# Values of a head pair in one chain of half-width products, latent sample scores in another

## The chip, the cores and the metric

The kernel runs on one core of a Trainium2 chip. The metric is the device time of one launch in microseconds; smaller is better. TensorE (PE) multiplies, PEld is its weight load, VectorE (DVE), ScalarE (ACT) and GpSimd (POOL) do the elementwise work, and SyncE (SP) issues the transfers. Each engine takes its instructions in a fixed order, and waits for semaphores where an operand comes from another engine.

## The reference

One inference step of a two-layer encoder in fp32, for 256 frames of a new stream ("prompt") and 64 frames of a running stream ("sample"), 320 columns together. Each layer is a SwiGLU block, a mixer stage and a second SwiGLU block, each followed by a layer norm. The mixer stage has two kinds of attention with eight heads of 64 values each, latent (A) and banded (B):

```python
# A, sample: 512 cached latent rows and the 64 new ones are keys and values
keys_c = jnp.concatenate([cache_ckv, ckv], axis=1)
s = (einsum('bqhc,bkc->bhqk', q_abs, keys_c) + einsum('bqhr,bkr->bhqk', q_rope, keys_r)) * MLA_SCALE
p = jax.nn.softmax(s, axis=-1)
o = einsum('bhqk,bkc->bqhc', p, keys_c)            # prompt: same, with a chunk mask
# B: own chunk of 64 and the 8 before it, with a learned relative bias
s = einsum('bqhd,bkhd->bhqk', q, k) * BAND_SCALE + bias
o = einsum('bhqk,bkhd->bqhd', softmax(s), v)
mix = (sigmoid(g_a) * (o_a @ w_pa) + sigmoid(g_b) * (o_b @ w_pb)) @ w_out
```

So per pair of heads there are scores, a softmax and values, for the sample (576 keys) and for the prompt (256 keys), in both A and B.

## The kernel before, in words

Activations lie with features on the 128 partitions and the 320 frames along the free dimension, as blocks of 128 features. Weights stream through SP's queue into staging tiles `wst`, and each is split into a high part `whi` (ACT, line 81) and a low part `wlo` (DVE, every sixth on POOL, line 83). A projection multiplies each 128 x 128 weight block three times (`mm3`: high by high, high by low, low by high), each a 128 x 320 product of type fp32r. They are by far the most instructions on TensorE, and are called weight products below.

Scores, transposes of probabilities and values are fp32 products. Heads come in pairs: head j of a pair owns partitions j*64 to j*64+63 of the results. Full-width products give 128 partitions at once (`sp`, the prompt scores, and `ss` in attention B, with zeros in Q to keep the heads apart). Half-width ones give 64 partitions, one head: the sample values (tile `so`, 64 columns), the prompt values (`po`, 256 and 128 columns) and, in attention A alone, the sample scores (`ss`, 288 columns, two halves b of two heads j each).

For each pair, `values_sample` transposes the sample's probabilities into PSUM tiles `st0`, `st1`, copies them to `pts` (ACT, line 586) and `ptn` (DVE, line 587) and multiplies: five products for each head, heads alternating. `hi` and `lo` (lines 123 and 130) then split the 64 columns into `oh` (ACT) and `ol` (DVE), the operands of the output projection. `values_prompt` does the same with `pt0`, `pt1`, `pt` (ACT line 566, DVE line 567) and four products, into 256 columns of the same `oh` and `ol`. That is six PSUM tiles of the tag "at" for a pair.

The program is written as a sequence of such steps, with projections between them. A list scheduler then sets each engine's order: it takes what it reckons to be ready, in order of priority, so products from different steps are mixed. What it sets is fixed before the run; on the chip each engine keeps to it and waits where its reckoning was wrong. Layer 0's mixer stage lies at about 265 to 505 us of the trace, layer 1's at 1030 to 1280. In each, B's four pairs come first (`values(0)` to `values(3)`), then A's four (`mla_pair`, `mla_scores`, `mvalues`). `mla_pair(i)` forms a pair's Q (a memset on POOL, DMAs of the rotary part, products on DVE) and K (copies on ACT and DVE); `mla_scores` multiplies them.

Of the kernel before, what the change touches and what calls it, by code (L numbers as in the profile page):

```python
# [23 lines left out]
PAST = 512  # L24
# [24 lines left out]
class WeightStream:  # L49


    def __init__(self, nc, dram, stage_pool, split_pool, ahead_dma, ahead_split):
        self.nc, self.dram = nc, dram
        self.sp, self.pp = stage_pool, split_pool
        self.ad, self.asp = ahead_dma, ahead_split
        self.order = []
        self.loaded = {}
        self.split = {}
        self.nl = self.ns = self.nlo = 0
# [42 lines left out]
class Model:  # L102
    def __init__(self, tc, a):
        self.tc, self.nc, self.a = tc, tc.nc, a


    def mm(self, out, lhsT, rhs, start, stop):
        self.nc.tensor.matmul(out, lhsT, rhs, start=start, stop=stop)  # L108

    def mm3(self, out, w, x, start, stop):  # L110
        self.mm(out, w[0], x[0], start, False)
# [341 lines left out]
class Mixer:  # L453
# [100 lines left out]
                nc.vector.tensor_scalar(pr[j][:, c0:c1], pr[j][:, c0:c1], st[:, 12 + i:13 + i], None, ALU.mult)  # L554
        return pr

    def values_prompt(self, pr, vp, i, o):
        nc, M = self.nc, self.M
        p0 = M.psum("at", "pt0")
        p1 = M.psum("at", "pt1")  # L560
        for j in range(2):
            nc.tensor.transpose(p0[:, j * 256:j * 256 + 128], pr[j][:, 256:384], M.ident)
            nc.tensor.transpose(p0[:, j * 256 + 128:j * 256 + 256], pr[j][:, 0:128], M.ident)
            nc.tensor.transpose(p1[:, j * 128:j * 128 + 128], pr[j][:, 128:256], M.ident)
        pt = self.tile([P, 768], F32, "pt", 2)
        nc.scalar.copy(pt[:, 0:512], p0)
        nc.vector.tensor_copy(pt[:, 512:768], p1[:, 0:256])
        ps = M.psum("at", "po")
        c = [slice(i * 128 + j * 64, i * 128 + j * 64 + 64) for j in range(2)]
        for j in range(2):  # L570
            M.mm(ps[j * 64:j * 64 + 64, 0:256], vp[0][:, c[j]], pt[:, j * 256:j * 256 + 256], True, False)
        for j in range(2):
            M.mm(ps[j * 64:j * 64 + 64, 128:256], vp[1][:, c[j]], pt[:, 512 + j * 128:640 + j * 128], False, True)
        M.hi(o[0][:, TS:T], ps[:, 0:256])
        M.lo(o[1][:, TS:T], ps[:, 0:256], o[0][:, TS:T])

    def values_sample(self, pr, vc, vs, i, o):

        nc, M = self.nc, self.M
        p0 = M.psum("at", "st0")  # L580
        p1 = M.psum("at", "st1")
        for t in range(4):
            nc.tensor.transpose(p0[:, t * 128:t * 128 + 128], pr[:, t * 128:t * 128 + 128], M.ident)
        nc.tensor.transpose(p1[0:64, 0:128], pr[:, 512:576], M.ident)
        pt = self.tile([P, 512], F32, "pts", 1)
        nc.scalar.copy(pt, p0)
        nc.vector.tensor_copy(M.ptn[0:64, :], p1[0:64, 0:128])
        ps = M.psum("at", "so")
        pairs = [(vc[t], pt[:, t * 128:t * 128 + 128]) for t in range(4)] + [(vs, M.ptn)]
        for t, (v, x) in enumerate(pairs):  # L590
            for j in range(2):
                r = slice(j * 64, j * 64 + 64)
                M.mm(ps[r, 0:64], v[:, r], x[:, r], t == 0, t == 4)
        M.hi(o[0][:, 0:TS], ps[:, 0:64])
        M.lo(o[1][:, 0:TS], ps[:, 0:64], o[0][:, 0:TS])

    def normalise_sample(self, pr, st, n):
        nc = self.nc
# [123 lines left out]
    def mla_pair(self, i):  # L722

        nc, M, l = self.nc, self.M, self.l
        pq = self.uq(i)
        Q = self.tile([P, 640], F32, "Q", 4)
        nc.gpsimd.memset(Q[96:128, 0:T], 0.0)
        nc.gpsimd.memset(Q[0:32, T:], 0.0)
        for j, (r, n) in enumerate(((64, 0), (32, 64))):
            t, g = divmod(2 * i + j, 4)  # L730
            c = slice(j * T, j * T + T)
            nc.sync.dma_start(out=Q[r:r + 32, c], in_=self.qr[t][g * 32:g * 32 + 32, :])
            nc.vector.tensor_tensor(Q[n:n + 64, c], pq[n:n + 64, :T], self.rq[n:n + 64, :], ALU.mult)
        w = [self.ws.next(("uk", l, i, k)) for k in range(2)]
        p0, p1 = M.psum("mm"), M.psum("mm")
        for k in range(2):
            M.mm3(p0, w[k], self.cc[k], k == 0, k == 1)
        for k in range(2):
            M.mm3(p1[:, :T], w[k], self.ckv[k], k == 0, k == 1)
        K = self.keys[i % 2]  # L740
        for k, r in zip(K, (slice(0, 64), slice(64, 128))):
            nc.scalar.copy(k[r, 0:PAST], p0[r, :])
            nc.vector.tensor_copy(k[r, PAST:], p1[r, 0:T])
        return Q, K

    def mla_scores(self, i, Q, K):
        nc, M = self.nc, self.M
        s = [M.psum("at", "ss") for _ in range(2)]
        for b in range(2):
            c = slice(b * 288, b * 288 + 288)  # L750
            for j in range(2):
                M.mm(s[b][j * 64:j * 64 + 64, 0:288], Q[:, j * T:j * T + TS], K[j][:, c], True, True)
        st = self.tile([P, 16], F32, "st", 8)
        pr = self.tile([P, 576], F32, "ps", 2)
        for b in range(2):
            nc.vector.tensor_reduce(st[:, b:b + 1], s[b][:, 0:288], AX.X, ALU.max)
        nc.vector.tensor_scalar(st[:, 2:3], st[:, 0:1], st[:, 1:2], -MLA_SCALE, ALU.max, ALU.mult)
        for b in range(2):
            nc.scalar.activation(pr[:, b * 288:b * 288 + 288], s[b][:, 0:288], AF.Exp, bias=st[:, 2:3], scale=MLA_SCALE,
                                 accum_out=st[:, 4 + b:5 + b])  # L760
        self.normalise_sample(pr, st, 2)
        sp = self.scores_prompt([Q[:, j * T + TS:j * T + T] for j in range(2)], K)
        for p in sp:
# [29 lines left out]
    def attention(self, pre):  # L793
        nc, M, l, a, ws = self.nc, self.M, self.l, self.a, self.ws
# [13 lines left out]
        Q = {}  # L808
        for i in range(2):
            Q[i] = self.band_q(*pre[2 * i])  # L810
            t, b = pre[2 * i + 1]
            self.band_k(i, t, ld[i][0], b)
        pv = [M.psum("at") for _ in rows]
        for i in range(NPAIR):
            ps = self.w_in("bv", i, "mm")
# [5 lines left out]
        vs = M.vsn  # L821
        nc.scalar.copy(vs[0:TS, :], pv[0][:TS, :])
        vp = [self.new_values(pv[t]) for t in (1, 2)]
# [6 lines left out]
        ob = [[self.tile([P, TR], F32R, f"o{n}{i}", 1) for n in "hl"] for i in range(NPAIR)]  # L830
# [5 lines left out]
        def values(i):  # L836
            prs, prp = S.pop(i)
            vc = ld[i][1]
            self.values_sample(prs, [vc[:, t * 128:t * 128 + 128] for t in range(4)], vs[:, i * 128:i * 128 + 128], i, ob[i])
            self.values_prompt(prp, vp, i, ob[i])  # L840

        def prep(i):
            ld[i] = self.band_load(i)
# [6 lines left out]
        scores(1)  # L850
        self.latent_kv()
        values(0)
        prep(3)
        scores(2)
        for j in range(3):
            self.latent_q(j)
        values(1)
        scores(3)
        for j in range(3, 6):
            self.latent_q(j)  # L860
        gb[0] = self.gate(1, 0)
        values(2)
        for m in range(1, 4):
            gb[m] = self.gate(1, m)
# [28 lines left out]
        vsm = M.vsn  # L893
        nc.scalar.copy(vsm[0:TS, :], pn[0][:TS, :])
        vpm = [self.new_values(pn[t]) for t in (1, 2)]
        H[1] = self.mla_pair(1)
        oa = [[self.tile([P, TR], F32R, f"o{n}{i}", 1) for n in "hl"] for i in range(NPAIR)]

        def mvalues(i):
            prs, prp = S.pop(i)  # L900
            c = slice(i * 128, i * 128 + 128)
            self.values_sample(prs, [v[:, c] for v in vcm], vsm[:, c], i, oa[i])
            self.values_prompt(prp, vpm, i, oa[i])

        mscores(1)
        ga[0] = self.gate(0, 0)
        mvalues(0)
        H[2] = self.mla_pair(2)
        mscores(2)
        ga[1] = self.gate(0, 1)  # L910
        mvalues(1)
        H[3] = self.mla_pair(3)
        mscores(3)
        ga[2] = self.gate(0, 2)
        mvalues(2)
        for m in range(3, 8):
            ga[m] = self.gate(0, m)
# [137 lines left out]
```

## Time and profile before

| | |
|---|---|
| median of 3 runs | 1546.58 us (1546.03 to 1548.86) |
| profiled execution | 1545.9 us, span 1544.1 us, granted clock 0.991 |
| busy, share of the span | PE 97%, PEld 94%, DVE 59%, ACT 48%, POOL 36% |
| PE idle, layer 0's mixer stage (265 to 505) | 7.0 of 240 us |
| PE idle, layer 1's mixer stage (1030 to 1280) | 5.2 of 250 us |

The span is what the trace covers; the rest of an execution's time lies around it. A row of the timeline has start, length (to the modelled end of the last of them), engine, line, operation, tile written <- tiles read, shape and the number of records merged into the row. Weight products overlap, so the time one takes is read from the start of the next, not from its length. Line 108 is the helper that issues all products, so they are told apart by their tiles. A product in fp32 has two records. Shapes with 128*64 are half width.

### The profile page before, as it was taken

To read this page: it belongs to the slowest core of one execution; us is meant where nothing else is said; L and a number is where in the kernel's file an instruction comes from. 1 tells how busy PE (TensorE), PEld (TensorE's weight loads), DVE (VectorE), ACT (ScalarE), POOL (GpSimd) and SP (SyncE) were. 2 spreads that over 40 slices of the span, in tenths; PEclk is the share of its full clock that TensorE was granted. 3 is DMA by queue.
4 is the path that set the end of the run, shared out by engine and by line. 5 is a ranking of instruction groups with operands and counts; after the bars stand their busy time and mean duration, and the time that the engine had idled before them with its cause. 6 is when DMAs were issued, how large, how long until landed. Compare 5 with 4: busy or idle time off the path is not lost. (4 is left out here: it accounts for less than half of the span.)

```text
span 1544.1 us, 26702 instructions
## 1 busy us (share of the span) xinstructions
PE 1499.4 (97%) x10207; PEld 1454.2 (94%) x10207; DVE 904.7 (59%) x1603; ACT 747.0 (48%) x1579; POOL 562.0 (36%) x602
## 2 busy tenths in 40 slices
PE   9999999999999899999999999999999999999996
PEld 9999999899898899999999999998998998899996
DVE  6333368775466994333784333786745579933345
ACT  5444345765453554443554443466634545544332
POOL 7222235232004683222483222452220146722234
PEclk9999999999999999999999999999999999999998
DMA  7554445844323435444435444457343334454441
GB/s 227 160 152 150 148 126 170 248 135 132 96 83 96 149 99 177 150 150 151 144 117 164 143 157 149 139 171 233 112 131 96 97 109 124 139 162 151 150 137 62
DMA packets 69920, 219.46 MB, mean 142 GB/s; under 512 B 8416, under 2 KB 17568, under 8 KB 69792
## 3 DMA queue, kind: packets, MB, share of 16 engines
q1 hardware_dynamic: 69792, 217.75, 45.5%
q8 instruction: 80, 1.31, 0.4%
q14 instruction: 48, 0.39, 0.1%
HBM read 211.74 MB, written 4.67 MB: 140 GB/s over the span
## 5 line engine op out<-in xcount | busy, mean ns | idle before, releaser
L83 DVE TENSOR_TENSOR wlo<-wst,whi 128x512 fp32r<-128x512 f32 (+1 forms) x640 | 470.8, 766 | 434.8 <-ACT whi L81 431.0
L81 ACT CAST whi<-wst 128x512 fp32r<-128x512 f32 (+1 forms) x768 | 436.9, 617 | 464.7 <-PE ps L108 193.5
L108 PE MATMUL ps<-xhi,whi 128*128 128x320 f32 x1760 | 548.6, 313 | 4.4 <-DVE fin L234 4.3
L108 PE MATMUL ps<-xlo,whi 128*128 128x320 f32 x1760 | 546.5, 311 | 6.0 <-DVE xlo L419 6.0
L108 PE MATMUL ps<-xhi,wlo 128*128 128x320 f32 x1760 | 545.5, 312 | 3.4 <-POOL wlo L83 3.2
L83 POOL TENSOR_TENSOR wlo<-wst,whi 128x512 fp32r<-128x512 f32 x128 | 175.2, 1369 | 472.4 <-ACT whi L81 452.0
L108 PEld LDWEIGHTS ps<-xlo,whi 128*128 128x128 f32 x1760 | 332.7, 189 | 7.0 <-DVE xlo L419 6.5
L108 PEld LDWEIGHTS ps<-xhi,whi 128*128 128x128 f32 x1760 | 332.7, 189 | 6.9 <-issue 6.2
L108 PEld LDWEIGHTS ps<-xhi,wlo 128*128 128x128 f32 x1760 | 331.8, 189 | 5.7 <-POOL wlo L83 3.5
L108 PE MATMUL ps<-hh,whi 128*128 128x320 f32 x704 | 217.8, 309 | 0.0
L108 PE MATMUL ps<-hh,wlo 128*128 128x320 f32 x704 | 217.5, 309 | 0.0
L108 PE MATMUL ps<-hl,whi 128*128 128x320 f32 x704 | 217.5, 309 | 0.0
L130 POOL TENSOR_TENSOR hl<-h,hh 128x320 fp32r<-128x320 f32 x88 | 85.6, 976 | 191.2 <-ACT hh L123 191.1
L108 PEld LDWEIGHTS ps<-hh,whi 128*128 128x128 f32 x704 | 132.1, 188 | 0.1
L108 PEld LDWEIGHTS ps<-hl,whi 128*128 128x128 f32 x704 | 132.1, 188 | 0.1
L108 PEld LDWEIGHTS ps<-hh,wlo 128*128 128x128 f32 x704 | 132.1, 188 | 0.0
L258 DVE TENSOR_TENSOR h<-silu,ps 128x320 f32<-128x320 f32 x79 | 38.3, 486 | 70.5 <-PE ps L108 67.3
L123 ACT CAST hh<-h 128x320 fp32r<-128x320 f32 x88 | 40.2, 457 | 54.8 <-DVE h L258 43.5
L108 PE MATMUL ps<-raw,whi 128*128 128x322 f32 x192 | 44.6, 319 | 1.1 <-DVE raw L311 1.0
L108 PE MATMUL ps<-rawl,whi 128*128 128x322 f32 x144 | 45.5, 316 | 0.0
L108 PE MATMUL ps<-rawh,wlo 128*128 128x322 f32 x144 | 45.2, 314 | 0.0
L331 POOL TENSOR_TENSOR d<-d,d 128x320 f32<-128x320 f32 x24 | 27.0, 1124 | 49.8 <-DVE d L361 29.3
(274 smaller groups left out, 2076.6 us busy)
## 6 DMA issues: line engine op xcount, KB each, us to landing
wst<-in_w_dram SPq DMA_DIRECT2D x382, 512.0 KB, 3.5
K<-in_ckT_dram SPq DMA_DIRECT2D x8, 256.0 KB, 4.6
vc<-in_cv_dram SPq DMA_DIRECT2D x8, 256.0 KB, 5.0
T<-in_E_dram SPq DMA_DIRECT2D x16, 128.0 KB, 4.2
xin<-in_x_dram SPq DMA_DIRECT2D x8, 160.0 KB, 6.0
out_kb_dram<-K SPq DMA_DIRECT2D x8, 160.0 KB, 3.6
out_vb_dram<-vt SPq DMA_DIRECT2D x8, 160.0 KB, 4.8
out_y_dram<-d SPq DMA_DIRECT2D x8, 160.0 KB, 1.8
```

The source lines that it names most:

```text
L81: self.nc.scalar.copy(hi[:, a:b], t[:, a:b])
L83: (self.nc.gpsimd if self.nlo % 6 == 0 else self.nc.vector).tensor_tensor(lo[:, a:b], t[:, a:b], hi.bitcast(F32)[:, a:b], ALU.subtract)
L108: self.nc.tensor.matmul(out, lhsT, rhs, start=start, stop=stop)
L123: self.nc.scalar.copy(out, src)
L130: eng.tensor_tensor(out, src, hi.bitcast(F32), ALU.subtract)
L258: nc.vector.tensor_tensor(h, s, pg[:, :T], ALU.mult)
L331: nc.gpsimd.tensor_tensor(S, d[0] if m == 1 else S, d[m], ALU.add)
```

## The change

`values_sample` and `values_prompt` become one function `values`. All eleven transposes of a pair come first, into three PSUM tiles (the prompt's 128-column ones share `st1` with the sample's last), then four copies, two on ACT and two on DVE, then 14 products into one tile `po`: 64 columns of sample and 256 of prompt. One `hi` and one `lo` of 320 columns follow. The products go through `run`: each is ordered behind the one before it, the first behind all four copies and behind the chain before; these orders bind the scheduler and set no semaphore. They have high priority. The four sample score products of `mla_scores` go through `run` too, the first behind all DMAs, products and copies of the pair's Q and K. Lines of the changed kernel are numbered 1 to 16 higher than before: products are at line 109, the copies at 589 to 592, `hi` and `lo` at 139 and 146.

```diff
+        self.tail = []
...
+    def order(self, ins, after):
+        self.tc.add_manual_dep(ins.ins, after.ins.name,
+                               mybir.DependencyInfo(mybir.DependencyClass.NoSync, mybir.DependencyReason.DATA), reason="order")
+
+    def run(self, after, products):
+
+        last = None
+        with self.tc.high_priority():
+            for p in products:
+                ins = self.mm(*p)
+                for x in ([last] if last else after + self.tail):
+                    self.order(ins, x)
+                last = ins
+        self.tail = [last]
...
-    def values_prompt(self, pr, vp, i, o):
+    def values(self, prs, prp, vc, vs, vp, i, o):
...
+        p0, p1 = M.psum("at", "st0"), M.psum("at", "st1")
+        for t in range(4):
+            nc.tensor.transpose(p0[:, t * 128:t * 128 + 128], prs[:, t * 128:t * 128 + 128], M.ident)
+        nc.tensor.transpose(p1[0:64, 0:128], prs[:, 512:576], M.ident)
         for j in range(2):
...
+            nc.tensor.transpose(p1[:, 128 + j * 128:256 + j * 128], prp[j][:, 128:256], M.ident)
+        p2 = M.psum("at", "pt0")
...
+        after = [nc.scalar.copy(ps, p0),
+                 nc.vector.tensor_copy(M.ptn[0:64, :], p1[0:64, 0:128]),
+                 nc.vector.tensor_copy(pt[:, 512:768], p1[:, 128:384]),
+                 nc.scalar.copy(pt[:, 0:512], p2)]
+        out = M.psum("at", "po")
+        new = []
+        for t in range(5):
             for j in range(2):
                 r = slice(j * 64, j * 64 + 64)
-                M.mm(ps[r, 0:64], v[:, r], x[:, r], t == 0, t == 4)
-        M.hi(o[0][:, 0:TS], ps[:, 0:64])
-        M.lo(o[1][:, 0:TS], ps[:, 0:64], o[0][:, 0:TS])
+                v, x = (vc[t], ps[:, t * 128:t * 128 + 128]) if t < 4 else (vs, M.ptn)
+                new.append((out[r, 0:TS], v[:, r], x[:, r], t == 0, t == 4))
+        for n, x0, w, q in ((0, 0, 256, TS), (1, 512, 128, TS + 128)):
+            for j in range(2):
+                c = i * 128 + j * 64
+                new.append((out[j * 64:j * 64 + 64, q:T], vp[n][:, c:c + 64], pt[:, x0 + j * w:x0 + j * w + w], n == 0, n == 1))
+        M.run(after, new)
+        M.hi(o[0][:, 0:T], out[:, 0:T])
+        M.lo(o[1][:, 0:T], out[:, 0:T], o[0][:, 0:T])
...
-    def mla_scores(self, i, Q, K):
+    def mla_scores(self, i, Q, K, after):
         nc, M = self.nc, self.M
         s = [M.psum("at", "ss") for _ in range(2)]
-        for b in range(2):
-            c = slice(b * 288, b * 288 + 288)
-            for j in range(2):
-                M.mm(s[b][j * 64:j * 64 + 64, 0:288], Q[:, j * T:j * T + TS], K[j][:, c], True, True)
+        M.run(after, [(s[b][j * 64:j * 64 + 64, 0:288], Q[:, j * T:j * T + TS], K[j][:, b * 288:b * 288 + 288], True, True)
+                      for b in (1, 0) for j in range(2)])
```

Three places show what the scheduler makes of it. The first is TensorE's order at B's third pair in layer 0, `values(2)`. The rows are an instruction's number, line, operation, tiles, size and count; `xhi`, `xlo` are blocks of the layer's input, `pts`, `ptn` and `pt` the transposed probabilities, `vc`, `vsn` and `vp` the values. Before, around the sample block:

```order
2182 L108 MATMUL ps<-xhi_83,whi 128x320
2183 L108 MATMUL so<-pts,vc 64x64 x8
2184 L108 MATMUL so<-ptn,vsn 64x64 x2
2185 L562 MATMUL pt_3970<-ident,pp 128x128
2186 L563 MATMUL pt_3970<-ident,pp 128x128
2187 L564 MATMUL pt_3971<-ident,pp 128x128
2188 L562 MATMUL pt_3970<-ident,pp 128x128
2189 L563 MATMUL pt_3970<-ident,pp 128x128
2190 L564 MATMUL pt_3971<-ident,pp 128x128
2191 L108 MATMUL ps<-xlo_91,whi 128x320
```

and, 28 weight products after those transposes, around the prompt block:

```order
2217 L108 MATMUL ps<-xhi_84,whi 128x320
2218 L108 MATMUL ps<-xlo_92,whi 128x320
2219 L108 MATMUL po<-pt,vp 64x256 x2
2220 L108 MATMUL po<-pt,vp 64x128 x2
2221 L108 MATMUL ps<-xhi_84,wlo 128x320
2222 L108 MATMUL ps<-xhi_85,whi 128x320
```

In the change, the transposes all stand together:

```order
2155 L109 MATMUL rms<-qss,ones 128x320
2156 L579 MATMUL st_3939<-ident,ps 128x128 x4
2157 L580 MATMUL st_3940<-ident,ps 64x128
2158 L582 MATMUL st_3940<-ident,pp 128x128 x2
2159 L585 MATMUL pt_3948<-ident,pp 128x128
2160 L586 MATMUL pt_3948<-ident,pp 128x128
2161 L585 MATMUL pt_3948<-ident,pp 128x128
2162 L586 MATMUL pt_3948<-ident,pp 128x128
2163 L109 MATMUL ps<-xlo_91,whi 128x320
```

and the chain follows them 21 weight products (the input's, rows 2163 to 2183) later:

```order
2183 L109 MATMUL ps<-xhi_82,whi 128x320
2184 L109 MATMUL po<-pts,vc 64x64 x8
2185 L109 MATMUL po<-ptn,vsn 64x64 x2
2186 L109 MATMUL ps<-xlo_90,whi 128x320
2187 L109 MATMUL ps<-xhi_82,wlo 128x320
2188 L109 MATMUL po<-pt,vp 64x256 x2
2189 L109 MATMUL po<-pt,vp 64x128 x2
2190 L109 MATMUL ps<-xhi_83,whi 128x320
```

The two half-width blocks, 34 rows apart before, are now two weight products apart, with no transposes between them; 21 weight products now stand between the last transpose and the chain, where 24 stood ahead of the sample block and 28 ahead of the prompt block.

The second place is TensorE's order at A's first pair in layer 0, where the sample scores `ss` lie among the output projection's products (`oh`, `ol`). Before:

```order
2420 L108 MATMUL ss<-K,Q 64x288
2421 L108 MATMUL ps<-oh_3163,whi 128x320
2422 L108 MATMUL ps<-ol_3164,whi 128x320
2423 L108 MATMUL ss<-K,Q 64x288
2424 L108 MATMUL ps<-oh_3163,wlo 128x320
2425 L108 MATMUL ss<-K,Q 64x288
2426 L108 MATMUL sp<-K,Q 128x256
2427 L108 MATMUL ss<-K,Q 64x288
2428 L108 MATMUL sp<-K,Q 128x128
2429 L108 MATMUL sp<-K,Q 128x256
2430 L108 MATMUL sp<-K,Q 128x128
2431 L108 MATMUL ps<-oh_3165,whi 128x320
```

In the change:

```order
2422 L109 MATMUL ps<-oh_3165,wlo 128x320
2423 L109 MATMUL ss<-K,Q 64x288
2424 L109 MATMUL ps<-oh_3159,whi 128x320
2425 L109 MATMUL ss<-K,Q 64x288 x3
2426 L109 MATMUL sp<-K,Q 128x256
2427 L109 MATMUL sp<-K,Q 128x128
2428 L109 MATMUL sp<-K,Q 128x256
2429 L109 MATMUL sp<-K,Q 128x128
2430 L109 MATMUL ps<-ol_3160,whi 128x320
```

The four score products, each by itself before, became one, a weight product, and three in a row, with the prompt scores `sp` behind them.

The third place is ACT's order at `values(2)` in layer 0, from the copy of the sample's transposed probabilities on. `rstd` belongs to a norm, `gt` to a gate, `pp` are exponentials of the fourth pair's prompt scores. Before:

```order
230 L586 COPY pts<-st_3947 128x512
231 L636 ACT_TABLE_LOAD
232 L636 ACTIVATE rstd<-rstd 128x320
233 L81 CAST whi<-wst 128x512 x2
234 L782 ACT_TABLE_LOAD
235 L782 ACTIVATE gt_4021<-ps 128x320
236 L123 CAST oh_3163<-so 128x64
237 L548 ACTIVATE pp,st<-pp,st 128x256
238 L548 ACTIVATE pp,st<-pp,st 128x128
239 L566 COPY pt<-pt_3970 128x512
240 L548 ACTIVATE pp,st<-pp,st 128x256
241 L548 ACTIVATE pp,st<-pp,st 128x128
```

In the change:

```order
228 L589 COPY pts<-st_3939 128x512
229 L647 ACT_TABLE_LOAD
230 L647 ACTIVATE rstd<-rstd 128x320
231 L564 ACT_TABLE_LOAD
232 L564 ACTIVATE pp,st<-pp,st 128x256
233 L564 ACTIVATE pp,st<-pp,st 128x128
234 L564 ACTIVATE pp,st<-pp,st 128x256
235 L564 ACTIVATE pp,st<-pp,st 128x128
236 L592 COPY pt<-pt_3948 128x512
237 L81 CAST whi<-wst 128x512 x2
238 L792 ACTIVATE gt_4009<-ps 128x320
239 L139 CAST oh_3163<-po 128x320
```

The gate's activation went behind the exponentials, all four of which now come ahead of the copy `pt`; the copy of `oh` for the sample ahead of them is gone.

More of the change, by code (lines that the diff above doesn't have):

```diff
@@ L104, in __init__ @@
         self.tc, self.nc, self.a = tc, tc.nc, a
+        self.tail = []
     def mm(self, out, lhsT, rhs, start, stop):
-        self.nc.tensor.matmul(out, lhsT, rhs, start=start, stop=stop)
+        return self.nc.tensor.matmul(out, lhsT, rhs, start=start, stop=stop)
+    def order(self, ins, after):
[10 more added lines that the diff above has]
+        self.tail = [last]
     def mm3(self, out, w, x, start, stop):
@@ L555, in softmax_prompt @@
         return pr
-    def values_prompt(self, pr, vp, i, o):
+    def values(self, prs, prp, vc, vs, vp, i, o):
         nc, M = self.nc, self.M
-        p0 = M.psum("at", "pt0")
-        p1 = M.psum("at", "pt1")
+        p0, p1 = M.psum("at", "st0"), M.psum("at", "st1")
+        for t in range(4):
+            nc.tensor.transpose(p0[:, t * 128:t * 128 + 128], prs[:, t * 128:t * 128 + 128], M.ident)
+        nc.tensor.transpose(p1[0:64, 0:128], prs[:, 512:576], M.ident)
         for j in range(2):
-            nc.tensor.transpose(p0[:, j * 256:j * 256 + 128], pr[j][:, 256:384], M.ident)
-            nc.tensor.transpose(p0[:, j * 256 + 128:j * 256 + 256], pr[j][:, 0:128], M.ident)
-            nc.tensor.transpose(p1[:, j * 128:j * 128 + 128], pr[j][:, 128:256], M.ident)
-        pt = self.tile([P, 768], F32, "pt", 2)
[L566 to L569, printed above, removed]
-        for j in range(2):
[L571 to L590, printed above, removed]
+            nc.tensor.transpose(p1[:, 128 + j * 128:256 + j * 128], prp[j][:, 128:256], M.ident)
@@ new lines, in values @@
+        p2 = M.psum("at", "pt0")
+        for j in range(2):
+            nc.tensor.transpose(p2[:, j * 256:j * 256 + 128], prp[j][:, 256:384], M.ident)
+            nc.tensor.transpose(p2[:, j * 256 + 128:j * 256 + 256], prp[j][:, 0:128], M.ident)
+        ps = self.tile([P, 512], F32, "pts", 1)
+        pt = self.tile([P, 768], F32, "pt", 2)
+        after = [nc.scalar.copy(ps, p0),
+                 nc.vector.tensor_copy(M.ptn[0:64, :], p1[0:64, 0:128]),
+                 nc.vector.tensor_copy(pt[:, 512:768], p1[:, 128:384]),
+                 nc.scalar.copy(pt[:, 0:512], p2)]
@@ L591, in values_sample @@
+        out = M.psum("at", "po")
+        new = []
+        for t in range(5):
             for j in range(2):
                 r = slice(j * 64, j * 64 + 64)
-                M.mm(ps[r, 0:64], v[:, r], x[:, r], t == 0, t == 4)
-        M.hi(o[0][:, 0:TS], ps[:, 0:64])
-        M.lo(o[1][:, 0:TS], ps[:, 0:64], o[0][:, 0:TS])
+                v, x = (vc[t], ps[:, t * 128:t * 128 + 128]) if t < 4 else (vs, M.ptn)
+                new.append((out[r, 0:TS], v[:, r], x[:, r], t == 0, t == 4))
+        for n, x0, w, q in ((0, 0, 256, TS), (1, 512, 128, TS + 128)):
+            for j in range(2):
+                c = i * 128 + j * 64
+                new.append((out[j * 64:j * 64 + 64, q:T], vp[n][:, c:c + 64], pt[:, x0 + j * w:x0 + j * w + w], n == 0, n == 1))
@@ L728, in mla_pair @@
         nc.gpsimd.memset(Q[0:32, T:], 0.0)
+        after = []
         for j, (r, n) in enumerate(((64, 0), (32, 64))):
@@ L731, in mla_pair @@
             c = slice(j * T, j * T + T)
-            nc.sync.dma_start(out=Q[r:r + 32, c], in_=self.qr[t][g * 32:g * 32 + 32, :])
-            nc.vector.tensor_tensor(Q[n:n + 64, c], pq[n:n + 64, :T], self.rq[n:n + 64, :], ALU.mult)
+            after.append(nc.sync.dma_start(out=Q[r:r + 32, c], in_=self.qr[t][g * 32:g * 32 + 32, :]))
+            after.append(nc.vector.tensor_tensor(Q[n:n + 64, c], pq[n:n + 64, :T], self.rq[n:n + 64, :], ALU.mult))
         w = [self.ws.next(("uk", l, i, k)) for k in range(2)]
@@ L741, in mla_pair @@
         for k, r in zip(K, (slice(0, 64), slice(64, 128))):
-            nc.scalar.copy(k[r, 0:PAST], p0[r, :])
-            nc.vector.tensor_copy(k[r, PAST:], p1[r, 0:T])
-        return Q, K
-    def mla_scores(self, i, Q, K):
+            after.append(nc.scalar.copy(k[r, 0:PAST], p0[r, :]))
+            after.append(nc.vector.tensor_copy(k[r, PAST:], p1[r, 0:T]))
+        return Q, K, after
+    def mla_scores(self, i, Q, K, after):
         nc, M = self.nc, self.M
         s = [M.psum("at", "ss") for _ in range(2)]
-        for b in range(2):
-            c = slice(b * 288, b * 288 + 288)
-            for j in range(2):
-                M.mm(s[b][j * 64:j * 64 + 64, 0:288], Q[:, j * T:j * T + TS], K[j][:, c], True, True)
+        M.run(after, [(s[b][j * 64:j * 64 + 64, 0:288], Q[:, j * T:j * T + TS], K[j][:, b * 288:b * 288 + 288], True, True)
+                      for b in (1, 0) for j in range(2)])
         st = self.tile([P, 16], F32, "st", 8)
@@ L838, in values @@
             vc = ld[i][1]
-            self.values_sample(prs, [vc[:, t * 128:t * 128 + 128] for t in range(4)], vs[:, i * 128:i * 128 + 128], i, ob[i])
-            self.values_prompt(prp, vp, i, ob[i])
+            self.values(prs, prp, [vc[:, t * 128:t * 128 + 128] for t in range(4)], vs[:, i * 128:i * 128 + 128], vp, i, ob[i])
         def prep(i):
@@ L901, in mvalues @@
             c = slice(i * 128, i * 128 + 128)
-            self.values_sample(prs, [v[:, c] for v in vcm], vsm[:, c], i, oa[i])
-            self.values_prompt(prp, vpm, i, oa[i])
+            self.values(prs, prp, [v[:, c] for v in vcm], vsm[:, c], vpm, i, oa[i])
         mscores(1)
```

## Prediction

> **What bounds the kernel now.** I read the engines' totals first, then the busy time in the two mixer stages, where all the edited code runs.
>
> ```profile
> span 1544.1 us, 26702 instructions
> PE 1499.4 (97%) x10207; PEld 1454.2 (94%) x10207; DVE 904.7 (59%) x1603; ACT 747.0 (48%) x1579; POOL 562.0 (36%) x602
> ```
> ```profile
> 265.00:505.00 240.00, 232.97 (x1642) 213.62 (x1641) 155.94 (x356) 131.73 (x312) 54.43 (x74) 1.00 0.45 136
> 1030.00:1280.00 250.00, 244.79 (x1719) 224.88 (x1718) 158.71 (x375) 137.47 (x325) 67.18 (x89) 1.00 0.46 139
> 298.00:312.00 14.00, 11.48 (x90) 9.84 (x89) 13.58 (x23) 9.98 (x25) 5.37 (x8) 1.00 0.67 178
> ```
>
> The columns behind the window are its length, then the busy time of PE, PEld, DVE, ACT and POOL, the granted clock, the DMA share and GB/s. TensorE is idle for only 7 and 5 us of these 240 and 250 us. So the time is TensorE's stream of instructions plus a few waits, and whatever shortens that stream shortens the run, if nothing new is waited for. The waits of both stages are short enough to list. Each row is the waiting tile, what it waited for, the total, the count and the longest:
>
> ```profile
> PE so L108 <- DVE ptn L587: 2.5, 1, 2.5
> PE ps L108 <- DVE mxl L132: 1.5, 1, 1.5
> PE ps L108 <- DVE wlo L83: 0.9, 1, 0.9
> PE ps L108 <- ACT oh L123: 0.5, 1, 0.5
> ```
> ```profile
> PE po L108 <- ACT pt L566: 0.5, 1, 0.5
> PE ps L108 <- ACT oh L123: 0.5, 1, 0.5
> PE so L108 <- DVE ptn L587: 0.5, 1, 0.5
> ```
>
> The first fence is layer 0, the second layer 1. A "busy" TensorE isn't one at its best rate, though. Start times show what a half-width product costs its neighbours:
>
> ```profile
> 430.48 0.31 PE L108 MATMUL ps<-xhi,wlo 128*128 128x320 f32 x1
> 430.62 0.31 PE L108 MATMUL ps<-xhi,whi 128*128 128x320 f32 x1
> 430.86 0.69 PE L108 MATMUL so<-pts,vc 128*64 128x64 f32 x16
> 431.38 0.29 PE L108 MATMUL so<-ptn,vsn 128*64 128x64 f32 x4
> 431.59 0.33 PE L562 MATMUL pt<-ident,pp 128*128 128x128 f32 x1
> 431.76 0.27 PE L563 MATMUL pt<-ident,pp 128*128 128x128 f32 x1
> 431.87 0.27 PE L564 MATMUL pt<-ident,pp 128*128 128x128 f32 x1
> ```
>
> An ordinary weight product follows the one before it after 0.14 to 0.15 us; the last one before the half-width block holds TensorE for 0.24 (430.62 to 430.86), 0.09 more. The first transpose behind the block takes 0.17 where the next takes 0.11, 0.06 more. The block itself, 20 records, takes 0.73. The profile keeps two records for each product, and a record of each head runs at the same time, so these are ten steps. The first eight take 0.52; I put 0.05 of that down to the entry, which makes a step 0.058, ten steps 0.58, and 0.15 (0.05 in, 0.10 out) the cost of the two ends. **A visit to half width costs about 0.30 us** here, beyond its products.
>
> ```profile
> 385.11 0.41 PE L108 MATMUL ps<-oh,whi 128*128 128x320 f32 x1
> 385.37 0.30 PE L108 MATMUL ps<-ol,whi 128*128 128x320 f32 x1
> 385.60 0.70 PE L108 MATMUL ss<-K,Q 128*64 128x288 f32 x2
> 386.23 0.41 PE L108 MATMUL ps<-oh,wlo 128*128 128x320 f32 x1
> 436.62 1.14 PE L108 MATMUL ss<-K,Q 128*64 128x288 f32 x8
> 437.69 0.70 PE L108 MATMUL sp<-K,Q 128*128 128x256 f32 x2
> ```
>
> Where a weight product comes next, it takes 0.26 (385.11 to 385.37, behind another visit), 0.11 more, so a visit between full-width products costs 0.09 + 0.15 + 0.11 = 0.35. The last two rows hold a second thing: one score product alone takes 0.63 us (385.60 to 386.23), four with the heads alternating 1.07. Taking off the 0.15 of the ends (of which the four, entered from half width, pay 0.10), a lone product is 0.48, and two of different heads share those 0.48.
>
> **The change, part by part.** TensorE executes the same products and transposes; their grouping changes.
>
> *Visits.* The order of before has 17 blocks that lead into transposes (the sample values), 17 that hold prompt values (four with paired scores right behind), and 16 lone score products: two heads times two halves in the first two latent pairs of each of two layers. That costs 17 x 0.30 + 33 x 0.35 = 16.6 us. The order of the change has 16 chains of values, 4 of them cut in two (by one full-width score product or two weight products), and 8 blocks of latent scores: each of those four pairs has one lone product, one weight product, then three in a row. That is 28 x 0.35 = 9.8. The difference is **-6.8 us**. Bounds: -5.9 if the ends cost 0.12 instead of 0.15, -7.6 at 0.18 (the rows round to 0.01).
>
> *Shared columns.* Per affected latent pair, four lone products at 0.48 become one lone, one pair and one lone: 1.92 becomes 1.44, times four pairs **-1.9**. Bounds: 0 if the row of three does not pair, -3.8 if the neighbour across the single weight product overlapped too; the fours at 436.62 are the nearest row, so I keep 1.9. The Trainium skill, "TensorE: Matmul & The Clock Gate", Part 3, says that weight loads overlap running products only where the row groups differ; both heads use all rows, so by it this term would be 0. The trace does not agree: four took 1.07 us where four lone ones would take 2.5.
>
> *One tile, one split.* Sixteen ACT copies of 64 columns and sixteen DVE subtractions go, their columns joining the 256-wide ones. Neither engine is what TensorE waits for on average (DVE 156 of 240 us), so I price this at 0; were DVE's whole saving on the path it would be 16 x 0.15 = 2.4.
>
> *Waits removed or moved.* In layer 0, the first band pair loses part of its 2.5 us:
>
> ```profile
> 299.07 0.69 PE L108 MATMUL so<-pts,vc 128*64 128x64 f32 x16
> ```
> ```profile
> 298.14 2.85 DVE L83 TENSOR_TENSOR wlo<-wst,whi 128x512 fp32r<-128x512 f32 x1
> 301.55 0.50 DVE L664 STREAM_SHUFFLE rr<-krz 128x320 f32<-128x320 f32 x1
> 301.95 0.27 DVE L587 COPY ptn<-st 64x128 f32<-64x128 f32 x1
> 304.71 2.14 DVE L637 RECIPROCAL rstd<-rstd 128x320 f32<-128x320 f32 x1
> ```
>
> The copy lands at 302.2 because it stands behind a 2.85 us weight subtraction and three others, and the change leaves that order on DVE. On TensorE six transposes (0.11 each) and nine weight products (0.147) now come ahead of the chain, so it arrives at 301.0, runs 16 records and waits from 301.5: 0.75 left, 1.75 saved. The last ACT copy lands at about 302.4, 0.1 later. Behind it the tile stays in use until the DVE subtraction of all 320 columns, which now stands behind that 2.14 us reciprocal and two weight subtractions; the second prompt-score product needs that PSUM slot, and I estimate 0.65 us for it. Net **-1.0**, between -2.5 and +0.5. In layer 1 the same chain comes about 2 us later than its copies; its waits of 0.5 and 0.5 go, but the slot wait can appear too: **-0.5**, between -1.0 and +0.5. At the end of the stage each layer's 0.5 us wait for oh goes: 16 and 11 weight products (2.4 and 1.6 us) that do not need the last pair now stand behind the chain. **-0.9**.
>
> *A wait added.* In the third band pair the ACT copy of the prompt weights is put behind a second table load and four exponentials, and the chain's second half behind that copy:
>
> ```profile
> 343.38 0.59 ACT L586 COPY pts<-st 128x512 f32<-128x512 f32 x1 [1.56 <-PE st L583]
> 343.98 1.28 ACT L636 ACT_TABLE_LOAD   x1
> 345.27 0.47 ACT L636 ACTIVATE rstd<-rstd 128x320 f32<-128x320 f32 x1
> 348.51 0.52 ACT L548 ACTIVATE pp<-pp,st 128x256 f32<-128x256 f32 x1
> 348.92 0.20 ACT L548 ACTIVATION_READ_ACCUMULATOR pp<-pp,st 128x1 f32 x1
> 349.02 0.40 ACT L548 ACTIVATE pp<-pp,st 128x128 f32<-128x128 f32 x1
> 349.31 0.19 ACT L548 ACTIVATION_READ_ACCUMULATOR pp<-pp,st 128x1 f32 x1
> 349.40 0.58 ACT L566 COPY pt<-pt 128x512 f32<-128x512 f32 x1
> ```
>
> From 343.38: copy 0.6, load 1.28, root 0.4, load 1.28, two heads' exponentials 2 x 0.89, copy 0.58 end at 349.3. TensorE's transposes start at 342.8; 11 x 0.11, 21 weight products at 0.147, the sample block 0.73 and two more products bring it to the prompt part at 348.4. It waits 0.9 us, 1.1 with the handover. Both layers have this order: **+2.2**, between 0 (if ACT comes to the pair earlier than before) and +4 (if the exponentials wait for DVE's maxima too). The other pairs have 20 to 28 weight products (2.9 to 4.1 us) between the last transposes and the chain, and at most four exponentials (1.8) and two copies (1.2) ahead on ACT, so 0 there.
>
> **Sum:** -6.8 - 1.9 - 1.0 - 0.5 - 0.9 + 2.2 = -8.9 us. The profiled execution took 1545.9 us (span 1544.1), the median of the three timed runs 1546.58, so I subtract from that and expect **1537.7 us**. With every term at its better end the time is 1546.6 - 7.6 - 3.8 - 2.5 - 1.0 - 0.9 - 0 = 1530.8, at its worse 1546.6 - 5.9 + 0.5 + 0.5 - 0.9 + 4 = 1544.8; they will not all fall on one side, and 1533.5 to 1542 holds this case.
>
> **Rivals.**
> *The project stage takes some back* (chance 0.16). Right after the mixers TensorE waited 0.9 for a weight's low part and 1.5 for mxl, both DVE: reaching that place earlier, TensorE would wait longer. For it: those two waits. Against: only DVE's work since the last pair, not all of its 156 us, has to be late. At 2 us a layer the time is 1541.7.
>
> *Every chain waits for its last copy* (0.10). The order has the chain behind four copies instead of one, and products start in order, so one late copy stops TensorE with all the weight products behind it. For it: the 2.5 us wait, and the third pair. Against: 2.9 us of cover elsewhere. At 0.5 us for each of 16 chains the gain is gone: 1545.7. The same page of the Trainium skill, Part 1, has the clock fall back after some 3.4 us without work; the 2.5 us stall lies in a window with a granted clock of 1.00, and no run here shows a longer one.
>
> *The single tile holds up the next pair* (0.07), the slower side. The one PSUM tile is held from the first sample product to the subtraction of all 320 columns, where two tiles were freed separately. The scores that take the slot start behind DVE's queue, where the reciprocal (2.1 us) and weight subtractions stand ahead. Below 0.55 us a pair the rest wins; above 0.75 it is slower; at 0.8 x 16 = 12.8 the time is 1550.5. Only the pair with the reciprocal right ahead speaks for it: seven of eight pairs a layer have longer until the slot is needed.
>
> *The chain saves no visits* (0.05): if the ends are paid where operands change (sample to prompt values, values to scores) rather than where the width does, only the 1.9 and the waits remain, 1546.6 - 2.1 = 1544.5. Against: in 436.62 the scores follow the prompt values with no such loss.
>
> **How the numbers follow.** The forecast has 0.62. A measurement of this kernel tells about 0.2%, 3.1 us, from no change, so faster means below 1543.5: forecast and first rival, with a little of the others, 0.80. Same: the second and fourth rivals, 0.13 (their better part counted as faster). Slower: 0.07. The range runs from 1533.5, which few of the forecast's terms can pass together, to 1544.6, so that the fourth rival is in; left out are the second and third and a small lower tail.
>
> **What would show it.** In the changed profile, the steps around a chain should read 0.24 ahead and 0.26 behind, once per chain, with no gap from sample to prompt values; score products in threes should take about 1.05 us; the 2.5 us wait for ptn should be below 1, and the third pair should wait about 1 us for ACT's prompt copy. The forecast is wrong if waits for those copies appear at many pairs, if scores wait for the low part of the values, or if the waits behind the mixers grow by what was saved.

## The result and the profile after

The changed kernel takes 1535.16 us, the median of six runs (1533.77 to 1536.8); the kernel before, beside it, 1546.3 us (six runs). The ratio is 0.9928, with a 95% interval of 0.9914 to 0.9942: 11 us less, between 9 and 13.

The first rows of the changed kernel's page:

```profile
span 1535.0 us, 26682 instructions
PE 1492.3 (97%) x10207; PEld 1454.5 (95%) x10207; DVE 900.1 (59%) x1587; ACT 744.3 (48%) x1563; POOL 564.5 (37%) x602
```

As many products as before, in a span 9.1 us shorter. The profiled execution took 1536.8 us, the longest of the six, so the traces show 9.1 of the 11. All of it lies in the mixer stages. I measure each from the first weight product behind the norm (the product that waits for `fin`) to the first product of the out projection (the one that reads `mxh`). The rows before, of layer 0 and then of layer 1:

```profile
266.97 0.39 PE L108 MATMUL ps<-xhi,whi 128*128 128x320 f32 x1 [1.67 <-DVE fin L234]
...
488.91 0.45 PE L108 MATMUL ps<-mxh,whi 128*128 128x320 f32 x2
...
1032.16 0.38 PE L108 MATMUL ps<-xhi,whi 128*128 128x320 f32 x1 [1.56 <-DVE fin L234]
...
1254.71 0.30 PE L108 MATMUL ps<-mxh,whi 128*128 128x320 f32 x1
```

and after:

```profile
267.13 0.39 PE L109 MATMUL ps<-xhi,whi 128*128 128x320 f32 x1 [1.67 <-DVE fin L250]
...
484.16 0.45 PE L109 MATMUL ps<-mxh,whi 128*128 128x320 f32 x2
...
1027.41 0.39 PE L109 MATMUL ps<-xhi,whi 128*128 128x320 f32 x1 [1.57 <-DVE fin L250]
...
1245.39 0.45 PE L109 MATMUL ps<-mxh,whi 128*128 128x320 f32 x2
```

Layer 0 went from 221.9 to 217.0 us, layer 1 from 222.6 to 218.0: together **-9.5**. In the same stretches the waits of TensorE went from 6.14 to 4.83 us, so -1.3 are waits and **-8.2 the stream itself**, the same products in fewer visits to half width.

A chain, at the third band pair of layer 0:

```profile
345.24 0.31 PE L109 MATMUL ps<-xhi,whi 128*128 128x320 f32 x1
345.48 0.69 PE L109 MATMUL po<-pts,vc 128*64 128x64 f32 x16
345.99 0.29 PE L109 MATMUL po<-ptn,vsn 128*64 128x64 f32 x4
346.21 0.42 PE L109 MATMUL ps<-xlo,whi 128*128 128x320 f32 x1
346.46 0.31 PE L109 MATMUL ps<-xhi,wlo 128*128 128x320 f32 x1
347.87 0.87 PE L109 MATMUL po<-pt,vp 128*64 128x256 f32 x8 [1.10 <-ACT pt L592]
348.67 0.41 PE L109 MATMUL ps<-xhi,whi 128*128 128x320 f32 x1
```

The steps at the ends are 0.24 ahead and 0.25 behind, as at a visit before. The pair is one of the four that the order cut in two, and its second half waits 1.10 us for ACT's prompt copy. What else waited, in layer 0 and then in layer 1:

```profile
PE ps L109 <- DVE mxl L148: 1.5, 1, 1.5
PE po L109 <- ACT pt L592: 1.1, 1, 1.1
PE ps L109 <- DVE wlo L83: 0.9, 1, 0.9
PE po L109 <- DVE ptn L590: 0.4, 1, 0.4
PE sp L109 <- DVE pp L636: 0.4, 1, 0.4
```
```profile
PE ps L830 <- ACT vt L827: 1.4, 1, 1.4
PE po L109 <- ACT pt L592: 1.1, 1, 1.1
PE ps L109 <- DVE mxl L148: 0.4, 1, 0.4
PE sp L109 <- DVE pp L636: 0.3, 1, 0.3
```

The waits for `oh` are gone, that for `ptn` fell from 2.5 to 0.4, and the two behind layer 0's mixers, `wlo` 0.9 and `mxl` 1.5, are what they were. The 0.4 us that a prompt-score product `sp` waits for `pp` in layer 0 is new.

The latent scores of the first pair:

```profile
384.70 0.70 PE L109 MATMUL ss<-K,Q 128*64 128x288 f32 x2
385.33 0.41 PE L109 MATMUL ps<-oh,whi 128*128 128x320 f32 x1
385.67 1.19 PE L109 MATMUL ss<-K,Q 128*64 128x288 f32 x6
386.79 0.70 PE L109 MATMUL sp<-K,Q 128*128 128x256 f32 x2
```

One alone takes 0.63 us, the three behind it 1.12. The weight product between them holds TensorE for 0.34, because it has a visit on either side.

### The profile page after: what moved, and what is told of

It is laid out like the page before. It is cut to its first block, busy times and chain, and to the rows that moved or that the text cites. A ratio compares the mean times of both kernels' runs of the same rounds, so it can differ in the third digit from the quotient of the medians.

```text
span 1535.0 us, 26682 instructions
## 1 busy us (share of the span) xinstructions
PE 1492.3 (97%) x10207; PEld 1454.5 (95%) x10207; DVE 900.1 (59%) x1587; ACT 744.3 (48%) x1563; POOL 564.5 (37%) x602
## 5 line engine op out<-in xcount | busy, mean ns | idle before, releaser
L83 POOL TENSOR_TENSOR wlo<-wst,whi 128x512 fp32r<-128x512 f32 x128 | 176.1, 1376 | 466.3 <-ACT whi L81 428.8
```

The costliest lines, as they stand in the source:

```text
L83: (self.nc.gpsimd if self.nlo % 6 == 0 else self.nc.vector).tensor_tensor(lo[:, a:b], t[:, a:b], hi.bitcast(F32)[:, a:b], ALU.subtract)
```

## Experiments

Median times come from four sets of runs, in which the kernel before took 1546.3, 1545.0, 1544.3 and 1545.2 us, so across sets the ratios compare better than the medians. The table has the two stages as well, measured as above in the profiled execution, split into waits and stream. In two executions, e1's and e9's, a long wait in layer 1 was followed by a granted clock of 0.50 inside the measured stretch; it adds 1.5 us to their stream, worked out under e1 and e9, and is left in the table.

| kernel | median, us | ratio to before (95%) | both stages, us | waits | stream |
|---|---|---|---|---|---|
| before | 1546.3 | | 444.5 | 6.1 | 438.4 |
| the change | 1535.2 | 0.9928 (0.9914-0.9942) | 435.0 | 4.8 | 430.2 |
| e1, values only | 1539.6 | 0.9966 (0.9956-0.9976) | 441.5 | 6.1 | 435.4 |
| e2, scores only | 1538.3 | 0.9960 (0.9944-0.9975) | 439.0 | 4.9 | 434.1 |
| e3, second head first | 1532.8 | 0.9922 (0.9906-0.9939) | 430.5 | 4.0 | 426.5 |
| e4, copy first | 1531.4 | 0.9909 (0.9889-0.9929) | 431.0 | 2.3 | 428.8 |
| e5, heads apart | 1539.8 | 0.9967 (0.9956-0.9978) | 440.7 | 4.5 | 436.3 |
| e6, extra visit | 1542.3 | 0.9985 (0.9973-0.9996) | 441.3 | 4.4 | 436.9 |
| e7, two tiles | 1534.0 | 0.9929 (0.9912-0.9946) | 435.4 | 5.2 | 430.2 |
| e8, e3 and e4 together | 1527.5 | 0.9886 (0.9869-0.9904) | 427.4 | 1.9 | 425.6 |
| e9, heads in twos | 1534.7 | 0.9930 (0.9914-0.9947) | 438.2 | 6.1 | 432.1 |

### One part at a time: e1 and e2

e1 is the change without the chain of scores:

```diff
-        M.run(after, [(s[b][j * 64:j * 64 + 64, 0:288], Q[:, j * T:j * T + TS], K[j][:, b * 288:b * 288 + 288], True, True)
-                      for b in (1, 0) for j in range(2)])
+        for b in range(2):
+            c = slice(b * 288, b * 288 + 288)
+            for j in range(2):
+                M.mm(s[b][j * 64:j * 64 + 64, 0:288], Q[:, j * T:j * T + TS], K[j][:, c], True, True)
```

> Only the values are merged into chains; the latent sample scores are issued as before, one by one. Of before's 50 half-width visits 36 are left: the 17 + 17 value blocks become 20, the 16 lone scores stay. Theory (a visit costs 0.30 to 0.35 us, waits as in the change): visits 17 x 0.30 + 17 x 0.35 - 20 x 0.35 = 4.0 us less, waits 1.4 us less (4.7 + 4.7 us in the two mixer stages became 3.5 + 4.4 with the change), together 5.4 us less than before, about 1541. Rival (the chain saves nothing of itself, only waits and shared columns count): 1.4 us less, about 1545.

Measured: 3.0 us less in the two stages, 2.9 of it stream, where 4.0 was expected; the median is 5 us lower, by the ratio's interval 3.7 to 6.8. The stages are burdened by something else. In this execution a wait for `vt` in layer 1, ahead of all chains, was 3.4 us (1.4 before), and behind it the granted clock was 0.50 (the third column from the right in the second fence):

```profile
1047.05 0.52 PE L832 MATMUL ps<-ident,vt 128*64 128x128 f32 x3 [3.42 <-ACT vt L829]
```
```profile
1047.80:1051.00 3.20, 3.20 (x12) 2.91 (x11) 1.72 (x5) 2.30 (x5) 1.96 (x2) 0.50 0.93 282
```

From the end of that wait the order is the same in both kernels: three transposes, four weight products, two records of `ss`, eight weight products. They take 4.18 us here (1047.05 to 1051.22) and 2.67 before (1049.10 to 1051.77). Without these 1.5 us the stream is 4.5 us lower, beside the theory's 4.0 and far from the rival's 0. Without the 2.0 us by which the wait for `vt` is longer, the waits are 2.0 lower, where 1.4 was expected.

e2 is the kernel before with only `mla_scores` changed (the last part of the diff, with `run`).

> Only the latent sample scores are issued as a chain; the values are as before. 42 visits are left of 50, and each of four latent pairs has one lone score, one pair, one lone instead of four lone ones. Theory: 8 x 0.35 + 4 x 0.48 = 4.7 us less than before, about 1541.6. Rival (two heads' products do not share columns' time, as weight loads would not overlap): 2.8 us less, about 1543.5. If both rivals hold, no difference.

Measured: stream -4.2 us, where the theory has -4.7 and the rival -2.8; the stages -5.5, because the first pair's wait for `ptn` happened to be 1.2 instead of 2.5. So two heads do share the time. With e1's slow stretch taken out, the two streams add up to -8.7, where the change has -8.2: the two parts are independent to within 0.5 us.

### What a visit costs: e6

```diff
+        new.append((out[:, 384:448], M.ident, pt[:, 0:64], True, True))
         for n, x0, w, q in ((0, 0, 256, TS), (1, 512, 128, TS + 128)):
```

The added product's result is not used.

> The change with one more product in each chain of values, between sample and prompt: full width, 64 columns, into an unused part of the tile. The order has 40 visits instead of 28, since four chains were cut already. Theory (a visit costs 0.35): its own two records 16 x 0.11 = 1.7 and 12 x 0.35 = 4.2, together 5.9 us more than the change, about 1541. Rival (the ends are paid where the operands change, which happens there anyway): 1.7 us more, about 1537.

Measured: stream +6.7 us against the theory's 5.9 and the rival's 1.7; the median is 7 us higher, by the ratios 8.8. A chain of this kernel, with the product in its middle:

```profile
363.76 0.29 PE L109 MATMUL po<-ptn,vsn 128*64 128x64 f32 x4
363.98 0.43 PE L109 MATMUL po<-pt,ident 128*128 128x64 f32 x2
364.35 0.87 PE L109 MATMUL po<-pt,vp 128*64 128x256 f32 x8
365.15 0.41 PE L109 MATMUL ps<-xhi,wlo 128*128 128x320 f32 x1
```

and an uncut chain, from e8:

```profile
344.27 0.29 PE L109 MATMUL po<-ptn,vsn 128*64 128x64 f32 x4
344.39 0.82 PE L109 MATMUL po<-pt,vp 128*64 128x256 f32 x8
345.14 0.41 PE L109 MATMUL ps<-xhi,whi 128*128 128x320 f32 x1
```

Uncut, the four `ptn` records take 0.12 and the eight prompt records 0.75. Cut, they take 0.22 and 0.80, and the added product holds TensorE for 0.37 where its own two steps are worth 0.11: 0.41 us for one change to full width and back. Sample to prompt values, new operands and a new region of the tile, costs nothing. The Trainium skill, "TensorEngine Tiling (Array Packing)", Tiling Modes, Key Properties, says that changing the tiling mode, not just the tile, drains TensorE. The trace agrees, and has the price that the page does not give.

Half width alone is not what costs. A transpose into 64 partitions among full-width ones (`st`, line 580, in the change) takes a step of 0.11, like its neighbours:

```profile
341.55 0.27 PE L580 MATMUL st<-ident,ps 128*64 128x128 f32 x1
341.65 0.38 PE L582 MATMUL st<-ident,pp 128*128 128x128 f32 x2
```

Six fp32r products of 128*64 at 404.03 to 405.41 take 0.22 to 0.24 each, as the 128*128 ones of 512 columns around them do. So the price belongs to the heads' fp32 products in one half of the partitions; which of their properties brings it, no run here separates.

### Do the heads have to alternate: e5 and e9

```diff
-        for t in range(5):
-            for j in range(2):
+        for j in range(2):
+            for t in range(5):
...
-        for n, x0, w, q in ((0, 0, 256, TS), (1, 512, 128, TS + 128)):
-            for j in range(2):
+        for j in range(2):
+            for n, x0, w, q in ((0, 0, 256, TS), (1, 512, 128, TS + 128)):
```

> The change, but each chain of values runs all products of head 0 first, then all of head 1, instead of the heads alternating. Same products, same number of visits (28). Theory (a record of each head runs at the same time, and only side by side): sample part 20 steps of 0.052 instead of 10 of 0.058, 0.46 us more, prompt part 8 steps instead of 4 pairs, 0.6 us more, together 16 x 1.05 = 17 us more than the change, about 1552. Rival (weight loads of products on the same rows do not overlap, so alternating gains nothing): no difference.

Measured: +6.1 us of stream, between the two, so both were wrong. The trace shows why. TensorE's order in this kernel has the prompt part as 256, 128, 256, 128 columns: head 0's two products, then head 1's. What started between 348.60 and 349.10 us, by groups (busy time, mean, idle time before):

```profile
L109 PE MATMUL po<-pt,vp 128*64 128x256 f32 x4 | 0.7, 404 | 0.7 <-ACT pt L592 0.7
```

All four 256-column records, those of both heads, started before any of 128 columns, though in the order head 0's 128-column product stands between them. The prompt part lost nothing. The sample part did:

```profile
346.26 0.73 PE L109 MATMUL po<-pts,vc 128*64 128x64 f32 x10
346.78 0.22 PE L109 MATMUL po<-ptn,vsn 128*64 128x64 f32 x1
346.83 0.22 PE L109 MATMUL po<-pts,vc 128*64 128x64 f32 x1
346.84 0.22 PE L109 MATMUL po<-ptn,vsn 128*64 128x64 f32 x1
346.89 0.46 PE L109 MATMUL po<-pts,vc 128*64 128x64 f32 x5
347.19 0.28 PE L109 MATMUL po<-ptn,vsn 128*64 128x64 f32 x2
347.39 0.41 PE L109 MATMUL ps<-xlo,whi 128*128 128x320 f32 x1
```

It took 1.13 us instead of 0.73. Head 0's `ptn` product is its last, yet records of `pts`, which can only be head 1's, run around it: head 1 started while some two products of head 0 were still to come. That is 0.4 us a chain, 6.4 for 16. The Trainium skill, "TensorE: Matmul & The Clock Gate", Part 3, has products start and end strictly in order; these records do not agree with it for products on different column halves.

e9 asks how far this reaches, with the sample products in twos:

```diff
-        for t in range(5):
-            for j in range(2):
+        for t, j in [(t, j) for g in ((0, 1), (2, 3), (4,)) for j in range(2) for t in g]:
```

> The change, but the sample products of a chain alternate in twos: two products of head 0, two of head 1, and so on, and the last of each. With all of one head first the sample part lost 0.4 us a chain, while the prompt part, two products of each head in a row, ran side by side as if it alternated. Theory (TensorE starts a product of the other head although one or two products of the first head stand ahead of it, and no more): no loss, within 0.5 us of the change in the two mixer stages. Rival (only the next product in the order is started early): the first product of each two runs alone, about 0.23 us a chain, 3.7 us more than the change.

Measured: the median is 1534.7, within the change's own runs. In the trace, the steps of all sample records sum to 10.97 us instead of 10.72 in the change, 0.25 for 16 chains. The stages read 3.2 longer, but 1.3 of that are waits and 1.5 the clock: a wait of 2.9 us for `vt` in layer 1 was followed by a granted clock of 0.50 from 1047.6 to 1050.8, and the row of products behind it, with nine weight products at its end, takes 4.33 us (1046.74 to 1051.07) instead of 2.81 in the change (1044.45 to 1047.26). The other 0.4 hold the 0.25. This execution took 1539.5 us, the other three at most 1534.9; by the median there is no loss. So a product of the other half is taken past two that stand ahead, and not past five.

### One tile or two: e7

```diff
-        out = M.psum("at", "po")
+        out, out2 = M.psum("at", "so"), M.psum("at", "po")
...
-        M.hi(o[0][:, 0:T], out[:, 0:T])
-        M.lo(o[1][:, 0:T], out[:, 0:T], o[0][:, 0:T])
+        for x, c in ((out, slice(0, TS)), (out2, slice(TS, T))):
+            M.hi(o[0][:, c], x[:, c])
+            M.lo(o[1][:, c], x[:, c], o[0][:, c])
```

> The change, but sample and prompt values of a chain go to two PSUM tiles, each with its own split into high and low part (64 and 256 columns), as before. Same chains and visits (28). Theory (neither ACT nor DVE sets the end there): within 1 us of the change. Rival (one tile and one split is part of the gain, or one long-held tile costs): 2.4 us more, or 1 us or more less.

Measured: stream equal, waits 0.4 more, the ratio 0.9929 against 0.9928; the median, from another set, is 1 us less, with overlapping runs. One tile and one split of 320 columns are neither gain nor loss here; the chain is what pays.

### What was left lying: e3, e4 and e8

e3 starts the score chain with the head whose keys are copied last:

```diff
-                      for b in (1, 0) for j in range(2)])
+                      for b in (1, 0) for j in (1, 0)])
```

> The change, but each pair's latent score chain starts with head 1, whose keys are copied last, instead of head 0. The order then has all four products in one row with no weight product between (24 visits instead of 28). Theory: 4 x 0.35 + 4 x 0.48 = 3.3 us less than the change, about 1531.9. Rival (the chain now waits on the chip for the last copy of the keys, and TensorE stands still with it): up to 0.4 us for each of 8 pairs, no gain.

Measured: stream -3.7 us, waits -0.8, no new wait for the copies of the keys; the median is 2.4 lower, by the ratios 0.9. The scheduler had put a weight product behind the first score product because it could place the first before the second's operand was ready; with the latest operand first, nothing splits the row.

e4 puts ACT's prompt copy of the third band pair ahead of the fourth pair's exponentials:

```diff
-        return pr, self.softmax_prompt(pb, 1.0)
+        return pr, pb
...
+                if behind:
+                    self.M.order(e, behind)
...
         M.run(after, new)
+        self.copied = after[3]
...
         values(2)
+        S[3] = (S[3][0], self.softmax_prompt(S[3][1], 1.0, self.copied))
```

> The change, but in each layer the fourth band pair's prompt exponentials are formed behind the third pair's values, ordered behind ACT's copy of the third pair's prompt probabilities. The copy is then ahead of the second table load and the four exponentials on ACT, and the chain is no longer cut by two weight products (26 visits). Theory: the 1.1 us wait of each layer goes and one visit of 0.35, 2 x 1.45 = 2.9 us less than the change, about 1532.3. Rival (the wait only moves: the fourth pair's values or the gates wait for the later exponentials): no gain, or up to 2 us more.

Measured: waits -2.6, stream -1.4, the median 3.7 lower, by the ratios 2.9. ACT, in this kernel:

```profile
341.03 0.59 ACT L591 COPY pts<-st 128x512 f32<-128x512 f32 x1 [1.56 <-PE st L581]
341.63 1.28 ACT L650 ACT_TABLE_LOAD   x1
342.93 0.47 ACT L650 ACTIVATE rstd<-rstd 128x320 f32<-128x320 f32 x1
343.30 0.57 ACT L594 COPY pt<-pt 128x512 f32<-128x512 f32 x1
```

and in the change:

```profile
341.80 0.59 ACT L589 COPY pts<-st 128x512 f32<-128x512 f32 x1 [1.56 <-PE st L579]
...
347.25 0.56 ACT L592 COPY pt<-pt 128x512 f32<-128x512 f32 x1
```

The copy ends 2.8 us behind the first one's start, where the change needed 6.0. No wait behind the moved copy took its place.

e8 has both edits.

> The change with both edits: latent scores start with head 1, and ACT's prompt copy of the third band pair goes ahead of the exponentials. 22 visits. If the two are independent, 3.3 + 2.9 = 6.2 us less than the change, about 1529, 17 less than before. If either only moves a wait, correspondingly less.

Measured: 1527.5 us, 0.9886 of before (0.9869 to 0.9904), 7.6 less than the change, in the stages as by the medians, and 6.5 by the ratios; 6.2 was expected. In the stages the two edits alone gave 4.5 and 4.0, so they nearly add up. This is the fastest kernel of the study. Its only wait in layer 0 from 300 to 490 us:

```profile
PE ps L109 <- DVE wlo L83: 0.9, 1, 0.9
```

## Why the prediction was right

1537.7 us was forecast and 1535.2 measured, inside the range and on the side that had 0.8. In the stages, on the traces, -8.9 stood against -9.5; the remaining 1.6 between traces and medians is that the profiled execution was a long one. That the sum came within 0.6 us is in part luck: the stream fell 0.5 us less than worked out (-8.2, not -8.7), and the waits 1.1 more (-1.3, not -0.2). By its terms:

- **Visits and shared columns**, -6.8 and -1.9, came to -8.2 of stream. The mechanism is shown by e6, at 0.41 us for one change of width instead of 0.35, the sharing by e2. Each part is within half a microsecond of its term: the values -4.5 where 4.0 was worked out (e1, without its slow stretch), the scores -4.2 where 4.7 was (e2). The bounds of the first term were added up wrong: 22 visits at 0.03 more or less give -6.2 and -7.5, not -5.9 and -7.6.
- **First pair, layer 0**, -1.0: measured -2.1, or -1.7 with the new wait of `sp`, the largest miss. The step that failed is the wait of 0.65 us for the PSUM slot, which does not appear in either layer. And less was left of the wait for `ptn`, 0.4 instead of 0.75. The chain arrived 0.8 later than worked out (301.85, not 301.0): the arrival was counted from products alone, without the new 0.4 us wait of `sp` ahead of it, for which the sum has no term, and a start of the stage 0.2 later. The copy of `ptn` came 0.7 later too, which takes back most of that; the rest is that the profile counts the wait from the modelled end of the sixteen records (0.69), the sum from 0.5. The copy is late for another reason than its place in the order. Before, it stood behind a weight subtraction of 2.85 us, but DVE does others in 0.69; in the change the long row is another, a scaling of 576 columns (L613) that took 2.54 us, against 0.50 before (L602). In both, the long row lies beside POOL's weight subtraction and rotary product (1.28 and about 0.86 us), which are about what it is longer by; no run moves POOL's work to settle it.
- **First pair, layer 1**, -0.5: both waits went, about -1.0; the wait for the slot did not appear here either.
- **End of the stage**, -0.9: the two waits for `oh` went, -0.9.
- **Third pair**, +2.2: 1.1 us in each layer, +2.2. ACT's rows are those named, in the order that the changed program has; e4 removed the wait by moving the copy alone.
- **One tile**, 0: 0 (e7).

The rivals: the project stage took nothing back, `wlo` 0.9 and `mxl` 1.5 in the change and 0.9 and 1.5 in layer 0 before; even with 17 us less, e8 waits 0.9 for `wlo`. Chains waited for late copies at the first and third pairs only. No pair waited for the single tile, with which e7 agrees. And the chain does save visits: e6 had 6.7 more, where that rival would have 1.7.

One sentence beside the second rival was wrong: that no run here shows a stall longer than 2.5 us. Outside the mixers there are some, in both kernels. One in the change, and the clock behind it (third column from the right, in the windows' row):

```profile
546.28 0.64 PE L109 MATMUL ps<-xlo,whi 128*128 128x320 f32 x1 [3.37 <-DVE xlo L435]
546.72 0.47 PE L109 MATMUL ps<-xhi,wlo 128*128 128x320 f32 x1
546.98 0.47 PE L109 MATMUL ps<-xhi,whi 128*128 128x320 f32 x1
```
```profile
546.00:549.00 3.00, 2.72 (x10) 2.72 (x11) 3.00 (x9) 1.26 (x5) 2.03 (x2) 0.50 0.57 175
```

Behind 3.4 us without work the granted clock is 0.50, and a weight product takes 0.27 us instead of 0.15. The Trainium skill, "TensorE: Matmul & The Clock Gate", Part 1, has the fall after some 3.4 us without work, as the second rival says. This row agrees, but a shorter stall was followed by it too, e9's of 2.9 us, while the kernel before kept 1.00 behind 2.9 us at 534. The mixers' waits in the change, at most 1.5 us once `fin` has come, left the clock at 1.00.

The ends within a block were 0.15 us, by an entry that I set at 0.05; e6's rows give 0.10 and 0.05, the same.

## What to carry to other kernels

When TensorE is the bound, price the change between full width and one head's half, not only the product: here 0.35 to 0.4 us each time, read from the start of the next instruction, since the busy time hides it. Group half-width products and let the halves alternate, and then look in the new order for what cuts the group: the first product of a row should be the one whose operand comes last, and the copies it waits for should not stand behind table loads. An edit that moves copies earlier or later is worth pricing on the engine that makes them; both waits that the change left were visible there before it ran. And read the granted clock before two streams are compared: in e1 it passed for 1.5 us of the edit.

## What the runs showed of the hardware

TensorE did not keep to the order of products on different column halves. Four records of 256 columns, two of each head, all started before those of 128 columns that stood between them in the order (e5), and groups of two for each head ran nearly as fast as single alternation (10.97 and 10.72 us for 320 records), while five in a row cost 0.4 us a chain. So that an engine keeps to its fixed order holds for TensorE only within a column half, as far as these records go. I had expected 17 us from heads apart and measured 6. Half width itself was free where transposes and fp32r products of 64 partitions stood among full-width ones (steps of 0.11 and 0.22 to 0.24), and cost 0.35 to 0.41 us where the heads' fp32 products did. And stalls of 3.4 us (e1) and 2.9 us (e9) cost 1.5 us more than themselves, by a clock of 0.50 behind them.
